# Hybrid decoder trunk: all input sums of the FFN's seven-product scheme emitted behind tile 1, and two more tiles per layer in that scheme

## Chip, core and metric

One core of a Trainium2 chip runs the whole program. The metric is device time in microseconds (us) for one launch, smaller is better.

## What is computed

Two layers, each a token mixer and a gated MLP, over 528 tokens of width 1024 (16 learned tokens are put in front of 512), in float32. The change touches the MLP:

```
h = h + ffn(rmsnorm(h));   out = rmsnorm(h) without the first 16 tokens
ffn(x): u = causal_dwconv3(x @ w_up) + b        # 1024 -> 2 x 2816
        gate, val = split(u)
        (silu(gate) * val) @ w_down             # 2816 -> 1024
```

## The kernel before

Data lie with features on partitions: a tile is 128 features by 528 tokens, worked on in two halves of 264 (in layer 1 two of 258, because the first tokens are dropped). Each float32 operand of a matrix product is split in two float32r parts, a high one (a ScalarE copy) and a low one (the rest), and each product is three matmuls: high by high, high by low, low by high. `split` (L420 to L427) makes the low part on VectorE by one subtraction, or, with `by_dma`, as a negated copy on ScalarE followed by a DMA from GpSimd's queue (POOL) that adds the source onto it.

The MLP of a layer has 22 FFN tiles. Tile j needs gate column block j and value column block 22 + j of `w_up`. In the plain scheme (`up_pair`, L1026) that is two units of 8 x 3 matmuls for each half, 96 in all. Tiles in `FAST` use `up_fast` (L1070) with `pair_products` (L377): a Winograd form of a 2 x 2 block product, in which seven products of 4 x 3 matmuls (84) take the place of eight. It needs four sums of the inputs, T1 to T4, which depend on the layer only, and sums of the four weight blocks, which each tile makes anew: the items `a` (blocks as they are), `b` and `c` (each 1024 columns, two additions of 512 columns apiece on VectorE, L292 to L296) and `d` (512 columns). The order of the seven products is B11, B21, T1, T2, B22, T3, T4.

The input sums are made by `sum_pair` (L1044), one call for each of four pairs of feature tiles. A call adds high and low parts back together for two feature tiles (L1049), makes T1 and T2 (L1055, L1056) and T3 and T4 (L1059, L1060), and splits each two of them with `by_dma` into `th` and `tl`. All four pairs are needed in the middle of product T1. Before, pair 0 is emitted behind tile 1, pairs 1 and 2 behind tile 2, pair 3 behind tile 3; the first fast tile is tile 4.

Tiles 0 and 1 run as one block of four units: first half of all four, then second half of all four. Emptying a tile means: copy out of PSUM and first tap (ScalarE), two more taps (VectorE, L1000), SiLU, a multiplication (L1022) and a split into `ah` and `al`. The tiles fall in five groups (`GROUPS`). The down projection of a group (8 row tiles, each two halves of 4 x 3 matmuls) runs inside the next group's fast tiles, as many rows in each as `DOWNS` says; the last group's down projection stands at the end of the layer, and of its first four units the products with the last activation tile are put last.

Working buffers `t` of the MLP are seven (`TM`, by `big`): a tile being emptied takes four, a `sum_pair` call four, of which the two that are split by DMA are free when that DMA has landed. `ah` and `al` have eight buffers (L1023). Weight tiles come through three `raw` buffers, are cut (`prep`, L265) three items ahead of the one taken, into four pairs `wh`, `wl`.

TensorE and SyncE run in the order of the program. On the other engines a planner in the framework puts ready instructions in order, by their place in the program, on its own costs; each queue then runs strictly in that order.

Of the kernel before, what the change touches and what calls it, by code (L numbers as in the profile page):

```python
# [19 lines left out]
KD = D // P  # L20
# [10 lines left out]
NFF = 22  # L31

GROUPS = ((0, 4), (4, 8), (8, 12), (12, 16), (16, 22))
FAST = range(4, 21)
DOWNS = ((), (2, 2, 2, 2), (2, 2, 2, 2), (2, 2, 2, 2), (2, 2, 2, 1, 1, 0))
TM = 7
Q0 = 12
MAXH = 2
# [55 lines left out]
def hybrid_trunk_kernel(ctx, tc, x, w_in, w_out, w_up, w_down, par, pre_in, lru_w, kon, msk, rope, out):  # L94
# [105 lines left out]
    raw_src, items = [], []  # L200
# [4 lines left out]
        group[f"x{j}"], group[f"y{j}"], group[f"s{j}"] = [M_LX + j], [M_LY + j], [M_RG + j]  # L205
    orders = [[m for k in o.split() for m in group[k]] for o in (ORDER, ORDER1)]

    def plain(src, kn, ring="raw"):
        raw_src.append((src, kn, ring))
        items.append(("p" if ring == "raw" else "q", len(raw_src) - 1, kn))  # L210

    for l in range(DEPTH):
        for m in orders[l]:
            plain(w_in[l, m], KD)
        for m in range(KD):
            plain(w_out[l, m], KD)

        for g, (k0, k1) in enumerate(GROUPS):
            rows = iter(range(KD))
            for i, j in enumerate(range(k0, k1)):  # L220
                down = [next(rows) for _ in range(DOWNS[g][i] if g else 0)]
                if j in FAST:
                    raw_src.extend((w_up[l, r], KD, "raw") for r in (j, NFF + j))
                    ri = len(raw_src) - 2
                    items.extend((k, ri, KD) for k in "ab")
                    for q, m in enumerate(down):
                        plain(w_down[l, m, :, slice(*GROUPS[g - 1]), :], 4, "rd")
                        if q == 0:
                            items.append(("c", ri, KD))
                    if not down:  # L230
                        items.append(("c", ri, KD))
                    items.append(("d", ri, KD))
                else:
                    plain(w_up[l, j], KD)
                    plain(w_up[l, NFF + j], KD)
        for m in range(KD):
            plain(w_down[l, m, :, k0:k1, :], k1 - k0)
    raws, ready, sums = {}, {}, {}
# [256 lines left out]
    def whole(hi, lo):  # L495
        return lambda t0, n: (hi[:, t0:t0 + n], lo[:, t0:t0 + n])
# [406 lines left out]
    def layer(l):  # L903
# [122 lines left out]
        def up_pair(j):  # L1026
            us = {}

            def ev(key, m):

                def f(i, t0, n, ps):
                    if key not in us:
                        us[key] = new_u()
                    u, c = us[key]
                    S.copy(u[:, 2 + t0:2 + t0 + n], ps[:, 0:n])
                    o = max(t0, c0)
                    tap(u, c, m, o, t0 + n, ps[:, o - t0:n])
                return f
            return [(None, ev("g", j), lambda: gate(j, us)), (None, ev("v", NFF + j), lambda: value(j, us))]
# [4 lines left out]
        def sum_pair(a):  # L1044

            y = []
            for k in (2 * a, 2 * a + 1):
                y.append(big())
                V.tensor_tensor(y[-1][:, 0:2 * hn], xh[:, k, h0:T].bitcast(F32), xl[:, k, h0:T].bitcast(F32), op=ALU.add)  # L1049
            (b11, b12), (b21, b22) = ((t[:, 0:hn], t[:, hn:2 * hn]) for t in y)  # L1050
            for i in (0, 2):
                t = big()
                p0, p1 = t[:, 0:hn], t[:, hn:2 * hn]
                if i == 0:
                    V.tensor_tensor(p0, b11, b12, op=ALU.subtract)  # L1055
                    V.scalar_tensor_tensor(p1, p0, -1.0, b22, op0=ALU.mult, op1=ALU.subtract)  # L1056
                    t2 = p1
                else:
                    V.tensor_tensor(p0, b22, b12, op=ALU.subtract)  # L1059
                    V.scalar_tensor_tensor(p1, t2, -1.0, b21, op0=ALU.mult, op1=ALU.subtract)  # L1060
                split(t[:, 0:2 * hn].rearrange("p (h t) -> p h t", t=hn), *(x[:, a, i:i + 2, 0:hn] for x in tsum),
                      by_dma=True)
# [7 lines left out]
        def up_fast(j, halves):  # L1070
            us = {k: new_u() for k in "gv"}
            ug, uv = (us[k][0][:, 2 + h0:2 + T] for k in "gv")

            def evac(what, ps):
                p = ps[:, 0:hn]
                if what == "c11":
                    S.copy(ug[:, 0:hn], p)
                elif what == "u":
                    S.copy(ug[:, hn:2 * hn], p)
                elif what == "q5":  # L1080
                    S.activation(uv[:, hn:2 * hn], p, AF.Copy, scale=-1.0)
                elif what == "c11b":
                    V.tensor_tensor(ug[:, 0:hn], ug[:, 0:hn], p, op=ALU.add)
                elif what == "c12":
                    V.tensor_tensor(ug[:, hn:2 * hn], ug[:, hn:2 * hn], p, op=ALU.add)  # L1085
                    u, c = us["g"]
                    tap(u, c, j, c0, T, u[:, 2 + c0:2 + T])
                    gate(j, us)
                elif what == "v":
                    V.tensor_tensor(uv[:, hn:2 * hn], uv[:, hn:2 * hn], p, op=ALU.subtract)  # L1090
                else:
                    S.activation(uv[:, 0:hn], p, AF.Copy, scale=-1.0)
                    u, c = us["v"]
                    tap(u, c, NFF + j, c0, T, u[:, 2 + c0:2 + T])
                    value(j, us)
            cut_at = (len(halves) + 1) // 2

            def between(i):
                for f in (halves[:cut_at], halves[cut_at:])[i]:
                    f()  # L1100
            pair_products(xs_fast, KD // 2, hn, evac, between)

        def down_halves(m, xs):

            w = []

            def f(t0, n):
                if not w:
                    w.append(take())
                ps = ps_mm.tile([P, 512], F32, tag="mm", name=nm("mm"))  # L1110
                product(w[0], xs, t0, n, range(len(xs)), ps, True, True)
                resid(m)(0, t0, n, ps)
            return [lambda t0=t0, n=n: f(t0, n) for t0, n in hd]

        for g, (k0, k1) in enumerate(GROUPS):
            rows = iter(range(KD))
            prev = [whole(*act[k]) for k in range(*GROUPS[g - 1])] if g else []
            for i, j in enumerate(range(k0, k1)):
                halves = [f for _ in range(DOWNS[g][i] if g else 0) for f in down_halves(next(rows), prev)]
                if j in FAST:  # L1120
                    up_fast(j, halves)
                else:
                    if j == 0:
                        run_units([u for i_ in range(2) for u in up_pair(i_)], xs_norm, hv, first=4)
                    elif j > 1:
                        run_units(up_pair(j), xs_norm, hv)
                    if j in (1, 2, 3):
                        for a in {1: (0,), 2: (1, 2), 3: (3,)}[j]:
                            sum_pair(a)

        def final(t0, n):
# [27 lines left out]
    with tc.manual_schedule(engines={mybir.EngineType.PE, mybir.EngineType.SP}):  # L1159
# [132 lines left out]
        for l in range(DEPTH):  # L1292
            layer(l)
# [106 lines left out]
```

## Time and profile before

| | us |
|---|---|
| median of 3 runs (lowest, highest) | 1287.32 (1286.71, 1287.97) |
| the profiled execution, its span | 1288.41, 1286.5 |
| TensorE busy | 1258.5 (98%) |
| VectorE busy | 988.6 (77%) |
| ScalarE busy | 752.0 (58%) |
| GpSimd busy | 79.5 (6%) |
| mean granted TensorE clock | 0.987 |

Engines are named PE (TensorE matmul), DVE (VectorE), ACT (ScalarE), POOL (GpSimd), SP (SyncE). Times within the run are from the start of the span. In a row, `out<-in` are the tiles' names, L is the line, and what stands in brackets or behind a second bar is idle time ahead of it with what ended it. Listed durations on DVE and ACT overlap a little: the next one starts 0.06 to 0.1 us before the end of the one ahead.

### The profile page before, as it was taken

Reading aid. Unit: us, or ns where it says so; the run is one execution under the profiler, and the core shown is the slowest. Engines: PE = TensorE matmul, PEld = TensorE weight load, DVE = VectorE, ACT = ScalarE, POOL = GpSimd, SP = SyncE. Lnnn points to the kernel's source line nnn. Section 1 sums busy time; section 2 is a strip of 40 time slices with the busy share of each in tenths; the row PEclk is TensorE's granted clock in tenths of the full one; section 3 lists DMA queues with packets and bytes.
Section 4 is the critical chain, followed back from the end, with each engine's and each line's share of the span. In section 5 each row is a group of like instructions: output and inputs, shape, how many; then the busy total and the mean of one; then the engine's idle time right before and its main releaser. Section 6 shows DMA issues by size and latency. Waiting matters only on the chain.

```text
span 1286.5 us, 25758 instructions
## 1 busy us (share of the span) xinstructions
PE 1258.5 (98%) x10244; PEld 1245.9 (97%) x10244; DVE 988.6 (77%) x1946; ACT 752.0 (58%) x1442; POOL 79.5 (6%) x179
## 2 busy tenths in 40 slices
PE   9999999999899999999999999999999999999997
PEld 8999999999899999999999999999989999999996
DVE  7987676468788888887588767764896888888865
ACT  6665555347666666666456645553684666666652
POOL 0000000001211111100000000000021111111000
PEclk8999999999899999999999999999998999999998
DMA  5322312324555445544232223122265555555422
GB/s 197 98 78 67 100 50 66 99 67 122 126 132 132 131 128 136 132 124 115 75 99 67 66 66 100 50 83 66 87 136 139 132 132 131 132 137 135 111 88 74
DMA packets 53240, 135.32 MB, mean 105 GB/s; under 512 B 5632, under 2 KB 12288, under 8 KB 53120
## 3 DMA queue, kind: packets, MB, share of 16 engines
q1 hardware_dynamic: 39424, 110.46, 27.5%
q0 software_dynamic: 12544, 21.06, 9.7%
q10 hardware_dynamic: 1152, 2.16, 0.5%
q8 instruction: 80, 1.31, 0.4%
q14 instruction: 40, 0.33, 0.1%
HBM read 110.51 MB, written 2.10 MB: 88 GB/s over the span
## 4 chain that ended last, share of the span: by engine, by line
PE 86%; DVE 6%; ACT 3%; DMA 3%; issue 1%; SPq 0%; POOL 0%; DVEq 0%; ACTq 0%; POOLq 0%
PE mm L130 63%; PE mx L130 23%; DMA tl<-t 2%; DVE t L1000 1%; PE mx L137 1%; DVE wl L427 1%; DVE t L567 1%; DVE t L1138 0%; DMA raw<-in_w_in_dram 0%; DVE sc L591 0%; ACT wh L421 0%; ACT th L421 0%; DMA mk<-in_msk_dram 0%; DVE t L870 0%; ACT sc L674 0%
## 5 line engine op out<-in xcount | busy, mean ns | idle before, releaser
L130 PE MATMUL mm<-xh,wh 128*128 128x264 f32 (+1 forms) x1424 | 417.9, 293 | 0.8 <-ACT xh L421 0.8
L130 PE MATMUL mm<-xl,wh 128*128 128x264 f32 (+1 forms) x1424 | 404.3, 284 | 0.7 <-DVE xl L427 0.3
L130 PE MATMUL mm<-xh,wl 128*128 128x264 f32 (+1 forms) x1424 | 403.4, 283 | 0.0
L130 PE MATMUL mm<-ah,wh 128*128 128x264 f32 (+2 forms) x960 | 273.2, 285 | 0.0
L130 PEld LDWEIGHTS mm<-xl,wh 128*128 128x128 f32 x1424 | 268.8, 189 | 3.7 <-issue 1.9
L130 PE MATMUL mm<-al,wh 128*128 128x264 f32 (+2 forms) x960 | 272.4, 284 | 0.0
L130 PE MATMUL mm<-ah,wl 128*128 128x264 f32 (+2 forms) x960 | 272.1, 283 | 0.0
L130 PEld LDWEIGHTS mm<-xh,wh 128*128 128x128 f32 x1424 | 268.5, 189 | 3.6 <-issue 2.0
L130 PEld LDWEIGHTS mm<-xh,wl 128*128 128x128 f32 x1424 | 268.6, 189 | 0.2 <-DVE wl L1195 0.2
L427 DVE TENSOR_TENSOR wl<-raw,wh 128x1024 fp32r<-128x1024 f32 (+2 forms) x168 | 182.5, 1088 | 82.2 <-ACT wh L421 81.7
L421 ACT CAST wh<-raw 128x1024 fp32r<-128x1024 f32 (+2 forms) x168 | 158.3, 942 | 149.2 <-PE mm L130 143.6
L130 PEld LDWEIGHTS mm<-ah,wh 128*128 128x128 f32 x960 | 182.0, 190 | 0.1
L130 PEld LDWEIGHTS mm<-al,wh 128*128 128x128 f32 x960 | 181.9, 189 | 0.1
L130 PEld LDWEIGHTS mm<-ah,wl 128*128 128x128 f32 x960 | 181.9, 189 | 0.0
L1000 DVE SCALAR_TENSOR_TENSOR t<-t,pr,t 128x528 f32<-128x528 f32 (+1 forms) x176 | 132.7, 757 | 11.1 <-ACT t L1005 5.1
L130 PE MATMUL mx<-th,wh 128*128 128x264 f32 (+1 forms) x408 | 117.2, 287 | 0.0
L130 PE MATMUL mx<-th,wl 128*128 128x264 f32 (+1 forms) x408 | 116.6, 286 | 0.0
L130 PE MATMUL mx<-tl,wh 128*128 128x264 f32 (+1 forms) x408 | 116.3, 285 | 0.0
L1005 ACT ACTIVATE t<-t,pr 128x528 f32<-128x528 f32 (+1 forms) x68 | 56.0, 823 | 58.5 <-DVE t L1085 56.5
L427 DVE TENSOR_TENSOR wl<-ss,wh 128x1024 fp32r<-128x1024 f32 x68 | 83.0, 1221 | 4.6 <-ACT wh L421 1.8
L425 POOL DMA_DIRECT2D wl<-rd x64 | 56.6, 884 | 448.6 <-ACT wl L424 384.4
L130 PEld LDWEIGHTS mx<-tl,wh 128*128 128x128 f32 x408 | 78.3, 192 | 0.0
(231 smaller groups left out, 2170.9 us busy)
## 6 DMA issues: line engine op xcount, KB each, us to landing
raw<-in_w_up_dram SPq DMA_DIRECT2D x88, 512.0 KB, 3.6
raw<-in_w_in_dram SPq DMA_DIRECT2D x52, 512.0 KB, 3.6
rd<-in_w_down_dram SPq DMA_DIRECT2D x64, 256.0 KB, 2.7
wl<-rd POOLq DMA_DIRECT2D x64, 256.0 KB, 3.6
raw<-in_w_out_dram SPq DMA_DIRECT2D x16, 512.0 KB, 3.5
raw<-in_w_down_dram SPq DMA_DIRECT2D x16, 384.0 KB, 3.1
hT<-in_x_dram SPq DMA_DIRECT2D x4, 528.0 KB, 5.4
t<-in_rope_dram ACTq DMA_DIRECT2D x8, 264.0 KB, 3.3
```

What stands on the lines that cost most here:

```text
L130: PE.matmul(o, a, b, start=start, stop=stop, **kw)
L137: PE.transpose(o, a, ident[0:n, 0:n])
L421: S.copy(hi, src)
L425: G.dma_start(lo, src, accum_op=ALU.add)
L427: V.tensor_tensor(lo, src, hi.bitcast(F32), op=ALU.subtract)
L567: V.tensor_tensor(o, a, b, op=ALU.mult)
L1000: V.scalar_tensor_tensor(c[:, 0:cn], u[:, i + c0:i + c0 + cn], pr[l][:, w + i:w + i + 1], c[:, 0:cn], op0=ALU.mult, op1=ALU.add)
L1005: S.activation(c[:, a - c0:b - c0], src, AF.Identity, bias=pr[l][:, C_FB + m:C_FB + m + 1], scale=pr[l][:, C_FW + 3 * m + 2:C_FW + 3 * m + 3])
```

## The change

Fast tiles become 3 to 21 (from 4 to 20). All four `sum_pair` calls are emitted behind tile 1. The weights of the plain tiles 1 and 2 are split with `by_dma`. The last group's rows of the fourth group's down projection go 2, 1, 1, 2, 1, 1 over tiles 16 to 21 instead of 2, 2, 2, 1, 1, 0.

```diff
-FAST = range(4, 21)
-DOWNS = ((), (2, 2, 2, 2), (2, 2, 2, 2), (2, 2, 2, 2), (2, 2, 2, 1, 1, 0))
+FAST = range(3, 22)
+DOWNS = ((), (2, 2, 2, 2), (2, 2, 2, 2), (2, 2, 2, 2), (2, 1, 1, 2, 1, 1))
+SENT = (1, 2)
...
-    def plain(src, kn, ring="raw"):
+    def plain(src, kn, ring="raw", by_dma=False):
         raw_src.append((src, kn, ring))
-        items.append(("p" if ring == "raw" else "q", len(raw_src) - 1, kn))
+        items.append(("q" if by_dma else "p", len(raw_src) - 1, kn))
...
-                        plain(w_down[l, m, :, slice(*GROUPS[g - 1]), :], 4, "rd")
+                        plain(w_down[l, m, :, slice(*GROUPS[g - 1]), :], 4, "rd", True)
...
-                    plain(w_up[l, j], KD)
-                    plain(w_up[l, NFF + j], KD)
+                    plain(w_up[l, j], KD, by_dma=j in SENT)
+                    plain(w_up[l, NFF + j], KD, by_dma=j in SENT)
...
-                    if j in (1, 2, 3):
-                        for a in {1: (0,), 2: (1, 2), 3: (3,)}[j]:
+                    if j == 1:
+                        for a in {1: (0, 1, 2, 3)}[j]:
                             sum_pair(a)
```

## Rows read from the trace of the kernel before

**Rows 1.** The page: busy time by engine, and the chain that ended last, by engine
```profile
PE 1258.5 (98%) x10244; PEld 1245.9 (97%) x10244; DVE 988.6 (77%) x1946; ACT 752.0 (58%) x1442; POOL 79.5 (6%) x179
...
PE 86%; DVE 6%; ACT 3%; DMA 3%; issue 1%; SPq 0%; POOL 0%; DVEq 0%; ACTq 0%; POOLq 0%
```
**Rows 2.** PE's waits, whole run: in total, times, longest
```profile
PE mm L130 <- DMA tl<-t: 9.0, 2, 4.8
PE mm L130 <- ACT th L421: 2.5, 2, 1.5
```
**Rows 3.** Timeline of PE, layer 0, tile 4: start, duration, [idle before]
```profile
324.19 0.28 PE L130 MATMUL mx<-xh,wh 128*128 128x264 f32 x1
...
329.41 0.39 PE L130 MATMUL mm<-th,wh 128*128 128x264 f32 x1 [1.04 <-ACT th L421]
334.03 0.59 PE L130 MATMUL mm<-tl,wh 128*128 128x264 f32 x1 [4.23 <-DMA tl<-t]
```
**Rows 4.** Timeline of PE, layer 1, tile 4
```profile
957.23 0.28 PE L130 MATMUL mx<-xh,wh 128*128 128x258 f32 x1
...
967.98 0.58 PE L130 MATMUL mm<-tl,wh 128*128 128x258 f32 x1 [4.78 <-DMA tl<-t]
```
**Rows 5.** The chain in order of time: start, duration, what
```profile
309.81 5.58 DMA tl<-t
330.23 3.75 DMA tl<-t
...
599.54 38.01 PE mm L130 x312
...
1228.60 37.09 PE mm L130 x312
```
**Rows 6.** Busy time by stretch: length, then engines, granted clock, DMA share, GB/s
```profile
293.30:333.30 40.00, 35.46 (x291) 35.04 (x289) 39.52 (x64) 32.42 (x61) 8.62 (x16) 0.99 0.59 140
...
334.03:339.24 5.21, 5.21 (x23) 5.21 (x24) 0.69 (x1) 1.29 (x3) 0.02 (x1) 0.50 0.61 103
360.20:376.20 16.00, 16.00 (x134) 16.00 (x134) 13.63 (x21) 9.99 (x17) 1.86 (x4) 1.00 0.51 133
568.80:582.00 13.20, 13.20 (x111) 13.20 (x110) 12.60 (x19) 8.58 (x14) 1.00 (x3) 1.00 0.43 117
599.40:611.00 11.60, 11.60 (x98) 11.60 (x97) 7.62 (x11) 7.05 (x13) 0.00 (x0) 1.00 0.45 137
967.98:974.12 6.14, 6.14 (x28) 6.14 (x29) 0.86 (x2) 1.28 (x3) 0.00 (x0) 0.50 0.71 134
```
**Rows 7.** Timeline of DVE, layer 0, tiles 0 to 4
```profile
294.47 1.56 DVE L1000 SCALAR_TENSOR_TENSOR t<-t,pr,t 128x528 f32<-128x528 f32 x2
...
299.18 0.71 DVE L1049 TENSOR_TENSOR t<-xh,xl 128x528 f32<-128x528 f32 x1
299.81 0.70 DVE L1022 TENSOR_TENSOR t<-t,t 128x528 f32<-128x528 f32 x1
...
306.61 0.42 DVE L1056 SCALAR_TENSOR_TENSOR t<-t,t 128x264 f32<-128x264 f32 x1
...
308.26 1.21 DVE L427 TENSOR_TENSOR wl<-raw,wh 128x1024 fp32r<-128x1024 f32 x1
309.39 0.68 DVE L292 TENSOR_TENSOR ss<-raw 128x512 f32<-128x512 f32 x1
...
328.14 0.43 DVE L1056 SCALAR_TENSOR_TENSOR t<-t,t 128x264 f32<-128x264 f32 x1
```
**Rows 8.** Timeline of ACT, layer 0, second half of tiles 0 and 1
```profile
292.25 1.05 ACT L421 CAST wh<-raw 128x1024 fp32r<-128x1024 f32 x1 [1.79 <-PE mm L130]
...
296.15 0.57 ACT L1005 ACTIVATE t<-mm,pr 128x264 f32<-128x264 f32 x1
```
**Rows 9.** The page's DMA issues: number, size of each, median us to landing
```profile
wl<-rd POOLq DMA_DIRECT2D x64, 256.0 KB, 3.6
```
**Rows 10.** Timeline of DVE, layer 0: the last low part of tile 21
```profile
615.88 0.71 DVE L427 TENSOR_TENSOR al<-t,ah 128x528 fp32r<-128x528 f32 x1 [0.75 <-ACT ah L421]
```

## Prediction

> **What bounds the kernel now.** I read the page's busy times and chain first. PE is busy 98% and is 86% of the chain [rows 1], so the end moves by matmuls left out and by PE's waits. PE's waits over the whole run come next. Nearly all of them are one event, twice: the wait for the DMA that finishes `tl`, 9.0 us, and just ahead of it the wait for `th`, 2.5 us [rows 2]. PE's timeline puts both in the first fast tile of each layer. Tile 4 starts at 324.19, reaches the last quarter of product T1, and goes on with `tl` of pair 3 at 334.03 [rows 3]; in layer 1 at 967.98, for a tile that started at 957.23 [rows 4]. Behind that wait, in which PE did nearly nothing, the table of stretches shows the granted clock at 0.50, the lower of the two levels (1.2 GHz), for 5.21 us in layer 0 and 6.14 us in layer 1 [rows 6]. What makes the sums late is in the first row of the same table: from 293.3 to 333.3 DVE is busy 39.52 us of 40, while ACT has 32.42 [rows 6]. So this stage is bound by DVE, then by the chain behind the last sum. From the end of pair 3's T2 (328.14 + 0.43 = 328.57) to the matmul at 334.03 it takes 5.46 us: ACT's two copies, the issue on POOL, and a transfer of 3.75 us [rows 3, 5, 7].
>
> **The change part by part.** I count against the profiled execution, 1288.41 us (span 1286.5); the median of the runs is 1.09 us less.
>
> *Tile 21.* It loses 12 of 96 matmuls. A run of 312 takes 38.01 us, so 0.1218 us each in layer 0, and 37.09 us, 0.1189 each, in layer 1 [rows 5]: 1.46 + 1.43 = 2.89 us off PE. The cover is DVE. A fast tile with two down rows (16.0 us of PE) costs DVE 13.63 us; one with one row (13.2 us) shows 12.60 [rows 6]. Tile 21 left DVE idle for four of its 11.60 us; now it has the load of its neighbours, and 0.5 us of slack. The last activation was there at 615.88 + 0.71 = 616.6 [rows 10]; tile 21 ended near 611.2 (96 matmuls behind 599.54, where the run starts [rows 5]), and the 60 matmuls put ahead of it last 7.3 us, to 618.5. A first tap over 528 columns instead of 264 takes some 0.3 of the 1.9 us left.
>
> The new order of down rows adds a wait. The last row now runs in tile 21, and until it is through, the four old activation tiles hold half of the eight `ah`/`al` buffers, so tile 20's activation has none until 12 matmuls (1.46 us) before tile 21 ends. Then a cast and a subtraction of 0.71 [rows 10] follow, at most 1.05 + 0.71 = 1.8 us [rows 8, 10], and it is needed 12 matmuls into the down projection. That is 2.9 us from release to need, less what is queued behind the waiting cast on ACT (tile 21's own copies). Bounds 0 and 1.46 us; I take 0.3 a layer, near the free end. Tails: 2.89 - 0.6 = 2.3 us gained.
>
> *Tile 3 and the sums together.* Tile 3 has no down rows, so a whole fast tile, 84 matmuls, lies between its use of pair 3 and tile 4's: 84 x 0.1218 = 10.23 us, and 9.99 in layer 1. The changed kernel breaks even if pair 3 lands at 334.03 - 10.23 = 323.8, in layer 1 at 957.99. PE itself would be there sooner: tile 3 starts 96 matmuls before 324.19, at 312.5, and needs pair 3 34 matmuls later, at 316.6.
>
> When does it land? DVE's list, by the pitch of starts, 0.08 under the listed durations [rows 7]: emptying tiles 0 and 1, eight taps of 0.74 and four operations of 0.63, 8.4; three pairs of 2 x 0.63 + 4 x 0.34, 7.9; pair 3 to its T2, 1.9; item `a` of tile 3, 1.1; item `b`, 2.3. That is 21.6 us from the first tap at 294.47, so 316.1, and with the 5.46 us behind it 321.6. Without item `b` in between it is 319.3; with tile 2's emptying ahead of the last sums (4.2 us more) it is 325.8. The buffers say the same by another way: a tap of tile 1 started at 296.15 only when the taps begun at 294.47 had freed a `t` [rows 7, 8], so seven are too few already. With four calls in a row, pair 3's last `t` has to wait for pair 0's landing, 309.81 + 5.58 = 315.39 [rows 5]; two operations and the 5.46 us make 321.6 too. I take 322.0, since ACT also gets 2 x 0.95 us of negated copies for tile 2's weights in this stretch. Gain against break-even: 1.8 us, in layer 1 (the same chain 633.95 us later) 2.0. PE's wait stays as long as it was, some 5.4 us, and I leave the slow stretch as it is.
>
> What is late next is DVE's backlog. Tile 3's DVE work grows from about 6.5 (two cuts and an emptying) to 13.63 less four additions of 0.4 for the down rows, 12.0; tile 2's two cuts, 2.3, go to the DMA. So DVE has 3.2 us more to do in the stretch that it fills, and only 2.4 us per tile to win back after it. I charge 1.0 a layer (0 to 3.2). Starts: 0.8 + 1.0 = 1.8 us gained.
>
> *Weights of tiles 1 and 2 by DMA.* Tile 2's gate weights are cast from 292.25 [rows 8]; the negated copy ends near 294.3, the issue is some 0.9, and a transfer of twice 256 KB takes between 3.6 (the row for one) and 7.2 [rows 9]: 297.9 to 302.4, against a need at 300.8 + 0.24. I cost it at nothing; uncovered it is up to 1.4 us a unit; tile 1's likewise. They also hold their `raw` buffer until the landing, so tile 3's second load starts up to 5 us later; its sums are not due before 315.
>
> A rule that speaks against this: the Trainium skill (SBUF — State Buffer, section "SBUF: two separate sides") says that a DMA from GpSimd's queue can't write its descriptors while VectorE holds the shared port in a 2-port mode. The trace has such DMAs inside the stretch where DVE is full, and they landed in 3.75 and 5.58 us [rows 5, 6], the second with weight loads beside it. By the rule each could be late by one DVE operation, 1.2 us, which would make the sum 2.4 us longer; by the rows nothing is added.
>
> **Sum.** 2.3 + 1.8 = 4.1 us: 1288.41 - 4.1 = 1284.3 profiled, 1283.2 as a median.
>
> **The rivals.**
>
> *The buffers give a second wait (slower).* The sums' first operations are ready early and come first in the program, so they take the seven `t`. Tile 2 can't be emptied until they let go, and tile 3 needs four more: its T2 goes into the bank whose first content has to be copied to a `t`. Once pair 3 has landed, DVE still owes tile 2's emptying, 4.2 us, and PE waits for it and a copy (0.4), 4.6 us a layer. For it: the tap at 296.15 [rows 8]. Against it: that DVE runs other work while buffers are short, 39.52 of 40 [rows 6]. It decides from about 2 us a layer, the gain of both parts. Time: starts 2 x 3.8 lost, tails 2.3 gained: 1292.6.
>
> *The sums come in time (faster).* Pair 3 at 319.3, 4.5 us better a layer; the wait shrinks to 2.7 us and the clock stays at 2.4 GHz. The slow stretches cost 5.21 - 24 x 0.1218 = 2.3 and 6.14 - 28 x 0.1189 = 2.8 us [rows 6], so 2 x 4.5 + 5.1 + 2.9 = 17 us: 1270.3. Against it: DVE and ACT would have to follow the ideal order.
>
> *POOL's queue comes late.* It now carries eight sums and four weight tiles in the same 30 us; tile 1's and 2's weights make PE wait 1.5 us a layer: 1286.2.
>
> *The tail gives nothing.* Tile 20's and 21's activations come late by what the matmuls save: 1286.
>
> *The sums don't move.* The planner may still run tile 2's emptying first; that is the end 325.8 of the forecast.
>
> **How the numbers follow.** Forecast 0.38 (its own range 1276 to 1291, landing from 319.3 to 325.8, the backlog 0 to 3.2, the tail 0 to 1.46); second wait 0.20; sums in time 0.13; POOL late 0.17; no gain at the tail 0.12. A difference of 0.2%, 2.6 us, is what a measurement of this kernel can tell: faster is below 1284.7, slower above 1289.9. Faster: 0.27 of the forecast, 0.13, 0.06 and 0.04, 0.50. Slower: 0.17 of the second wait, 0.03 of POOL, 0.03 of the others, 0.23. Same: 0.27. The range 1272 to 1292 leaves out about half of the two outer rivals.
>
> **What would show it.** Right: PE has 48 matmuls less; its longest wait is still one for `tl`, now in tile 3, ended near 322 and 956; tile 4 starts near 329 to 331; the down projection at the layer's end follows tile 21 without a gap over 0.5 us. Wrong: a PE wait that ACT's copies out of PSUM end (second wait); pair 3 before 320 with the clock at full behind it; waits in tile 1 or 2 for `wl`; a wait for `ah` or `al` of tile 20 or 21. If both waits are gone and the time still is no better, the reading of the tails fails.

## The result, and the profile after

The changed kernel takes 1298.43 us in the median of three runs (1296.53 to 1299.26); the kernel before takes 1287.32. The ratio is 1.0083, with a 95% interval of 1.0061 to 1.0106. The change makes the kernel slower by some 11 us. The forecast was 1283.2, in a range from 1272 to 1292, so it failed in sign and in range. The profiled execution is the shortest of the three, 1296.53 us with a span of 1294.7; it is 8.1 us above that of the kernel before, while the medians are 11.1 apart.

Busy times and chain of the changed kernel, to be read beside [rows 1]:
```profile
PE 1258.4 (97%) x10196; PEld 1243.8 (96%) x10196; DVE 998.7 (77%) x1974; ACT 763.2 (59%) x1450; POOL 86.2 (7%) x187
...
PE 86%; DVE 6%; DMA 3%; ACT 3%; issue 2%; POOL 0%; SPq 0%; DVEq 0%; ACTq 0%; POOLq 0%
```
The 48 matmuls are gone, but PE is busy as long as before: fewer instructions, more of them at a lower clock. The 6.8 us more at half the clock (end of this section) make up at most 3.4 us of the 5.8 that 48 matmuls take; what makes up the rest stays open. PE's waits over the whole run say where (in total, times, longest), against [rows 2]:
```profile
PE mm L131 <- ACT t L1006: 8.5, 4, 3.1
PE mm L131 <- DMA wl<-raw: 5.5, 4, 1.8
PE mm L131 <- DMA tl<-t: 4.1, 2, 2.9
```
Two waits, for `tl` and `th`, were 11.5 us; now three are 18.1. The first is for a PSUM bank: PE can't write until ACT has copied the bank's content to a `t` buffer. The second is for the weights that the DMA now finishes. The third is the old wait for pair 3. PE's timeline puts them in order, in layer 0 and, in the last three rows, in layer 1:
```profile
310.10 0.39 PE L131 MATMUL mm<-xh,wl 128*128 128x264 f32 x1 [0.98 <-DMA wl<-raw]
...
320.57 0.59 PE L131 MATMUL mm<-xh,wh 128*128 128x264 f32 x1 [3.14 <-ACT t L1006]
...
324.39 0.39 PE L131 MATMUL mm<-th,wh 128*128 128x264 f32 x1 [0.81 <-ACT t L1006]
...
327.34 0.59 PE L131 MATMUL mm<-tl,wh 128*128 128x264 f32 x1 [1.20 <-DMA tl<-t]
...
957.91 0.39 PE L131 MATMUL mm<-xh,wh 128*128 128x258 f32 x1 [3.08 <-ACT t L1006]
...
961.68 0.58 PE L131 MATMUL mm<-th,wh 128*128 128x258 f32 x1 [1.46 <-ACT t L1006]
...
967.22 0.58 PE L131 MATMUL mm<-tl,wh 128*128 128x258 f32 x1 [2.93 <-DMA tl<-t]
```
Pair 3 is there at 327.3 and 967.2, where the forecast had 322 and 956. The table of stretches, for the first and the last row of [rows 6]:
```profile
293.30:333.30 40.00, 33.87 (x247) 32.72 (x246) 31.98 (x54) 29.44 (x52) 8.97 (x14) 0.91 0.67 147
...
958.70:972.40 13.70, 9.31 (x42) 8.69 (x41) 9.62 (x14) 8.85 (x18) 2.44 (x2) 0.50 0.79 177
```
DVE, busy for 39.52 of the 40 us before, is busy for 31.98. It is no longer what bounds the stage, and the stage still got longer. And TensorE has the lower of its two levels (1.2 GHz) for 13.7 us in one piece in layer 1, from 0.8 us behind the first bank wait to 5 us behind the wait for pair 3. Outside the start and the end of the run, the clock record holds 17.1 us at that level before and 23.9 us after.

### The profile page after: what moved, and what is told of

Its sections match the earlier page's. It is cut to its first block, busy times and chain, and to the rows that moved or that the text cites. A ratio compares the mean times of both kernels' runs of the same rounds, so it can differ in the third digit from the quotient of the medians.

```text
span 1294.7 us, 25732 instructions
## 1 busy us (share of the span) xinstructions
PE 1258.4 (97%) x10196; PEld 1243.8 (96%) x10196; DVE 998.7 (77%) x1974; ACT 763.2 (59%) x1450; POOL 86.2 (7%) x187
## 3 DMA queue, kind: packets, MB, share of 16 engines
q0 software_dynamic: 13696, 25.25, 11.3%
## 4 chain that ended last, share of the span: by engine, by line
PE 86%; DVE 6%; DMA 3%; ACT 3%; issue 2%; POOL 0%; SPq 0%; DVEq 0%; ACTq 0%; POOLq 0%
PE mm L131 60%; PE mx L131 24%; DMA tl<-t 2%; DMA wl<-raw 1%; PE mx L138 1%; DVE wl L428 1%; DVE t L568 1%; DVE t L1001 1%; DMA raw<-in_w_in_dram 0%; DVE t L1139 0%; DVE t L1050 0%; DVE sc L592 0%; ACT wh L422 0%; DVE t L871 0%; ACT sc L675 0%
## 5 line engine op out<-in xcount | busy, mean ns | idle before, releaser
L131 PE MATMUL mm<-xh,wh 128*128 128x264 f32 (+1 forms) x1328 | 393.6, 296 | 7.0 <-ACT t L1006 6.2
L131 PE MATMUL mm<-xh,wl 128*128 128x264 f32 (+1 forms) x1328 | 379.1, 285 | 5.5 <-DMA wl<-raw 5.5
L131 PE MATMUL mm<-xl,wh 128*128 128x264 f32 (+1 forms) x1328 | 379.4, 286 | 0.4 <-DVE xl L428 0.3
L131 PEld LDWEIGHTS mm<-xh,wh 128*128 128x128 f32 x1328 | 253.0, 190 | 10.3 <-ACT t L1006 6.6
L131 PEld LDWEIGHTS mm<-xh,wl 128*128 128x128 f32 x1328 | 252.9, 190 | 6.5 <-DMA wl<-raw 6.3
L131 PEld LDWEIGHTS mm<-xl,wh 128*128 128x128 f32 x1328 | 253.1, 191 | 3.4 <-issue 1.9
L131 PE MATMUL mx<-th,wh 128*128 128x264 f32 (+1 forms) x456 | 131.2, 288 | 1.2 <-DVE t L1091 1.2
L131 PE MATMUL mx<-th,wl 128*128 128x264 f32 (+1 forms) x456 | 130.4, 286 | 0.0
L131 PE MATMUL mx<-tl,wh 128*128 128x264 f32 (+1 forms) x456 | 130.0, 285 | 0.0
L131 PEld LDWEIGHTS mx<-th,wh 128*128 128x128 f32 x456 | 87.3, 191 | 1.8 <-DVE t L1091 1.8
```

The source lines that it names most:

```text
L131: PE.matmul(o, a, b, start=start, stop=stop, **kw)
```

## The experiments

Times are medians; the ratio is to the kernel before on the same chip, with its 95% interval. The waits are PE's, in us over the run: for weights (`wl`, by the DMA's or DVE's finish), for a bank (ACT's copy to `t`), and for sums (`th`, `tl`). early_own2_tail also waits 2.7 us for ACT's copies of another bank (L1077), the others at most 1.0; the kernels in which tile 3 takes seven products wait 1.0 to 1.2 us for DVE at a third (L1091). The last column is the time at the lower clock level between start and end.

| kernel | us | ratio | weights | bank | sums | low clock |
|---|---|---|---|---|---|---|
| before | 1287.3 | 1 | 0 | 0 | 11.5 | 17.1 |
| changed | 1298.4 | 1.0083 [1.0061, 1.0106] | 5.5 | 8.5 | 4.1 | 23.9 |
| tail_only | 1285.2 | 0.9977 [0.9967, 0.9986] | 0 | 0 | 11.9 | 13.7 |
| start_only | 1297.9 | 1.0083 [1.0069, 1.0096] | 5.5 | 9.6 | 3.2 | 27.3 |
| sent_only | 1309.4 | 1.0157 [1.0134, 1.0179] | 13.4 | 0 | 11.2 | 37.5 |
| sent1_only | 1294.1 | 1.0049 [1.0033, 1.0064] | 3.3 | 0 | 11.7 | 23.9 |
| no_sent | 1295.7 | 1.0061 [1.0047, 1.0074] | 0 | 10.7 | 7.8 | 23.9 |
| no_tile3 | 1299.4 | 1.0084 [1.0070, 1.0098] | 13.3 | 6.7 | 0 | 27.3 |
| neither | 1283.9 | 0.9964 [0.9950, 0.9977] | 0 | 11.2 | 0 | 13.7 |
| sums_only | 1287.1 | 0.9995 [0.9986, 1.0005] | 0 | 11.3 | 0 | 17.1 |
| sums_own2 | 1276.7 | 0.9913 [0.9899, 0.9928] | 1.8 | 0 | 0 | 0 |
| no_sent_own2 | 1289.0 | 1.0010 [1.0000, 1.0019] | 8.1 | 0 | 7.0 | 20.5 |
| own_gate_tail | 1279.5 | 0.9929 [0.9915, 0.9942] | 0 | 6.3 | 0 | 13.7 |
| tail_pair3early | 1279.5 | 0.9935 [0.9920, 0.9950] | 0 | 2.3 | 2.3 | 6.8 |
| tail_0112 | 1283.0 | 0.9959 [0.9945, 0.9973] | 0.6 | 2.7 | 3.1 | 13.7 |
| early_own2_tail | 1281.4 | 0.9951 [0.9939, 0.9964] | 0.6 | 2.2 | 0 | 10.2 |
| sums_own2_tail | 1274.1 | 0.9897 [0.9883, 0.9911] | 1.9 | 0 | 0 | 3.4 |

### Is the tail's part right?

tail_only is the kernel before with tile 21 and its down rows alone; start_only is the changed kernel without them.
```diff
-FAST = range(4, 21)          # tail_only, against before
+FAST = range(4, 22)
-DOWNS = (..., (2, 2, 2, 1, 1, 0))
+DOWNS = (..., (2, 1, 1, 2, 1, 1))
-FAST = range(3, 22)          # start_only, against the change; DOWNS as before
+FAST = range(3, 21)
```


> The kernel before with only the tail of the change: fast tiles 4 to 21, down rows 2, 1, 1, 2, 1, 1; input sums and weights as before. Theory T (the tails gain what the forecast counted, 24 matmuls less a small charge): 2.3 to 2.9 us under the kernel before, 1284.5 to 1285.0. Rival (tile 20's and 21's activations come late by what is saved): within 1 us of the kernel before. If T holds, all of the loss, and 2 to 3 us more, belongs to the starts of the MLPs.

> The change without tile 21: tile 3 by seven products, all sums behind tile 1, both tiles' weights sent. Theory (the tail's 2.6 us are separate from the start's loss): the changed kernel's ratio 1.0083 and 2.6 us more, 1300 to 1303 us on a kernel before of 1288, with the same waits in tiles 2 to 4 as the changed kernel. Rival (tile 21 lost its gain inside the change, since its sums or copies come at a layer's end that is late): 1297 to 1299.5.

Alone it gives 2.6 us, as the theory had it. Inside the change the medians don't show it: start_only's 1297.9 is the rival's figure. But the intervals (1.7 and 2.9 us each way) don't exclude it, and the trace of the changed kernel shows it against the one before. In layer 0 all work is 3.7 us late at tile 6 (it starts at 368.06, before at 364.38) and 2.4 us late behind tile 21, where layer 1's FFN starts. In layer 1 it is 9.6 us late at tile 6 (1007.85, before 998.20) and 8.2 at the end. That is 1.2 and 1.4 us gained. start_only, which has neither gain, also has 3.4 us more at the lower clock than the changed kernel, so the two don't differ by the tail alone. So the loss lies in the start of each layer, and it is some 13.5 us there by the medians (10.9 in the profiled execution).

### The sent weights, alone and in the change

```diff
+SENT = (1, 2)                # sent_only, against before; sent1_only: SENT = (1,)
...
-                    plain(w_up[l, j], KD)
+                    plain(w_up[l, j], KD, by_dma=j in SENT)
...
-SENT = (1, 2)                # no_sent, against the change
+SENT = ()
```


> The changed kernel with the weights of tiles 1 and 2 split on VectorE again. Theory B (seven t buffers: the sums hold them, tile 2 is emptied late, PE waits for PSUM banks, then for pair 3): the waits for wl go (5.5 us in the trace, and the slow stretch of 3.4 us behind the one in layer 1), the waits ended by ACT's copies stay or grow by the two cuts that DVE gets back: 1290 to 1294, still slower than before. Rival W (the late weights push everything behind them, and the rest follows from that): back to 1284 to 1287, waits for banks under 3 us in all.

> The kernel before with only the weights of tiles 1 and 2 split by DMA. Theory W: PE waits for wl as in the changed kernel, some 2.7 us a layer, and nothing gives it back: 1291 to 1294. Theory B: the same waits, but tile 2's two cuts (2.3 us) leave the full DVE stretch, so pair 3 lands up to 2.3 us earlier and the wait for tl shrinks by part of it: 1286 to 1290.

> The kernel before with only tile 1's weights finished by the accumulating transfer; tile 2's stay with the vector engine. With both tiles' weights sent, the time rose by 21.6 us. Theory (tile 2's are the dear ones: its raw buffers are held by tile 1's transfers, its copies start late and its matmul waits 5 us a layer, with the low clock behind it): 1288 to 1293 us, waits for wl of at most 2 us a layer. Rival (the transfers themselves are dear, each unit the same): half of it, 1297 to 1301 us.

Taken out of the change they give 2.7 us, which the intervals don't tell from nothing; 1295.7 is above what either side had expected. Put into the kernel before, they cost 20 us, more than either theory had; tile 1's alone cost 6.5 (1294.1, 1 us above its theory's range). PE's waits in sent_only:
```profile
PE mm L131 <- DMA wl<-raw: 13.4, 4, 5.3
PE mm L131 <- DMA tl<-t: 8.0, 2, 4.3
```
The relief of DVE bought next to nothing: PE's wait for `tl` was 9.0 and is 8.0, and in sent1_only it is 9.1. The same part costs 20 us in one place and 3 in the other, so the parts aren't additive.

### Both taken back

no_tile3 and neither undo tile 3's seven products in the change, the second one the sent weights as well.
```diff
-FAST = range(3, 22)          # no_tile3 and neither
+FAST = range(4, 22)
-SENT = (1, 2)                # neither only
+SENT = ()
```


> The changed kernel with tile 3 back in eight products; sums, sent weights and tile 21 as in the changed kernel. Theory (tile 3 is the dear part also beside ring buffers and sent weights): 2.9 us of matmuls more, but the kernel with the sums alone was at 1287, tile 21 gives 2.6 back and the sent weights cost 2.7 when the sums are early, so 1285 to 1290 us against 1298. Rival (the sent weights are as dear as they were alone, 21.6 us, whenever tile 3 does not hide their lateness behind its own wait): 1296 to 1306.

> The changed kernel with both taken back, tile 3 by seven products and the sent weights; sums behind tile 1 and tile 21 by seven products stay. Taking back one of them alone gave at most 2.7 us. Theory (the two delays lie beside each other: either alone holds the sums' stage up by about as much as both): both taken back give 12 to 15 us, 1283 to 1287 us, with only the wait for t L1006 of the kernel that moves the sums alone. Rival (they add up as measured one by one, 2.7 and nothing): 1294 to 1298.

Tile 3 taken back alone gives nothing (no_tile3's theory failed, its rival's range held), the sent weights alone 2.7 us, both together 15 us (1.0083 to 0.9964). So each of the two is enough to make the start late by about as much as both. With neither, tile 3 costs 12.5 us (no_sent against neither); with tile 3 in eight products, the sent weights cost 15 (no_tile3 against neither). A single-part undo, read by itself, would have acquitted both. no_tile3 shows why the weights are so dear. Its chain in order of time, ahead of the wait in tile 2 (start, duration, what):
```profile
299.07 4.61 DMA wl<-raw
...
303.73 3.52 DMA raw<-in_w_up_dram
...
308.87 0.96 ACT wl L425
...
310.11 0.15 POOL wl L426
```
ACT's timeline at the same place:
```profile
307.27 1.06 ACT L422 CAST wh<-raw 128x1024 fp32r<-128x1024 f32 x1 [1.14 <-DMA raw<-in_w_up_dram]
308.23 0.64 ACT L1018 ACTIVATE t<-t 128x528 f32<-128x528 f32 x1
308.77 1.05 ACT L425 ACTIVATE wl<-raw 128x1024 fp32r<-128x1024 f32 x1
```
And PE's timeline, at the matmul that needs the transfer:
```profile
315.72 0.59 PE L131 MATMUL mm<-xh,wl 128*128 128x264 f32 x1 [4.79 <-DMA wl<-raw]
```
There are three `raw` buffers. A sent tile keeps its own until the accumulating transfer has landed (299.07 + 4.61 = 303.68), so the next weight load starts at 303.73; in the kernel before, the load in that place started at 294.58:
```profile
294.58 0.33 SPq L249 DMA_DIRECT2D raw<-in_w_up_dram  x1
```
The cast that needs this load waits on ACT, and in the order that the planner wrote for ACT the negated copy of tile 2's second weight tile stands behind that cast. So the transfer that PE waits for is issued at 310.11. In the changed kernel, whose load in that place starts at 301.85, ACT's order in this stretch has one whole-tile cast less, the negated copy starts at 304.19, and PE waits 0.98 us instead of 4.79.

### The sums and the buffers

sums_only moves the four sums of the kernel before behind tile 1, and nothing else. sums_own2 empties tile 2 into the buffers `rd` (made wide enough for it) and `ss`, which are idle then, instead of the ring of seven `t`.
```diff
-                    if j in (1, 2, 3):
-                        for a in {1: (0,), 2: (1, 2), 3: (3,)}[j]:
+                    if j == 1:                                # both
+                        for a in (0, 1, 2, 3):
...
-            u, c = big(), big()
+            u, c = (own(tag, 2, ...) if tag else big() for _ in range(2))   # sums_own2
...
-                        us[key] = new_u()
+                        us[key] = new_u({"g": "rd", "v": "ss"}[key] if j == 2 else None)
```


> The kernel before with only the four input sums emitted behind tile 1; the first fast tile is still tile 4, so pair 3 is needed 11.7 us later than in the changed kernel. Theory B: pair 3 lands near 322 to 327, so the wait for tl (4.2 and 4.8 us) goes, but tile 2 is emptied as late as in the changed kernel and tile 3's units wait for banks, 3 to 7 us a layer: 1283 to 1292, with waits ended by ACT's copies of PSUM in tile 3. Rival (the early sums are free when nobody needs them early): both waits and the slow stretches behind them go, 1270 to 1276.

> The kernel with the four sums behind tile 1 and the first fast tile 4, with one edit: tile 2 is emptied into buffers of its own (the two rd and the two ss, which nothing else uses yet), not into the seven t. Theory B (tile 2's buffers come behind the sums' in the ring of t, so its PSUM banks stay full): the waits of 5.5 and 6.3 us at tile 3's start go, pair 3 is in time anyway, the clock stays at full: 11 us of waits and some 5 us of slow clock less, 1269 to 1273. Rival Q (not the buffers: DVE and ACT are full, and the copies out of PSUM stand behind the sums' work in any case): waits of 3 us or more a layer stay, 1281 to 1287.

The sums alone change nothing: the wait for `tl` is gone and one for a bank, as long, has come. PE's longest wait in sums_only, and the copy on ACT that ends it:
```profile
PE mm L130 <- ACT t L1005: 11.3, 2, 6.0
```
```profile
317.44 0.57 ACT L1005 ACTIVATE t<-mm,pr 128x264 f32<-128x264 f32 x1 [0.66 <-DMA tl<-t]
```
The copy out of PSUM has no `t` until a transfer of the sums lands and lets one go. The row shows 0.66 us of that; the rest lies in the order of ACT's queue, which has tile 2's copies behind the sums. Its first copy, in sums_only and, with buffers of its own, in sums_own2:
```profile
316.40 0.38 ACT L1035 COPY t<-mm 128x264 f32<-128x264 f32 x1 [0.17 <-issue]
```
```profile
304.02 0.38 ACT L1035 COPY rd<-mm 128x264 f32<-128x264 f32 x1 [0.70 <-PE mm L130]
```
PE's longest wait in this stage of sums_own2 is then
```profile
PE mm L130 <- DVE wl L427: 1.5, 2, 0.8
```
and the time falls by 10.3 us, with the clock at its upper level from the start of the run to its end part. The theory's 1269 to 1273 was too good by 4 us; no single wait that is left in this stage is over 0.8 us, and they are mostly for casts on DVE and ACT.

### Tile 3 by itself

no_sent_own2 is no_sent with the gate half of tile 2 in `rd` (`ss` is used by a fast tile 3). own_gate_tail is the same with tile 3 in eight products.
```diff
-                        us[key] = new_u()
+                        us[key] = new_u("rd" if j == 2 and key == "g" else None)   # both
-FAST = range(3, 22)
+FAST = range(4, 22)                                                            # own_gate_tail
```


> The changed kernel without the DMA-split weights (tile 3 fast, all sums behind tile 1), with tile 2's gate half emptied into the two rd buffers. Theory B: the waits of 5.2 and 6.1 us for a bank in tile 3 shrink to under 2 us; pair 3 is needed near 316 and lands by DVE's list at 319 to 323, so a wait for tl of 3 to 6 us stays, with its slow stretch: 1285 to 1291. Rival Q: no change, 1294 to 1297.

> The kernel of 1289.0 us (no sent weights, all sums behind tile 1, tile 2's gate half emptied into buffers of its own, tile 21 by seven products) with one thing changed: tile 3 goes back to eight products. Theory (tile 3 asks for its casts and for the sums some 10 us before the vector engine has them, 8.1 us of waits for wl and 7.0 for tl and the low clock behind them): without it 1274 to 1279 us, though 24 x 0.12 = 2.9 us of matmuls are added. Rival (the value half, still emptied into the ring, is what costs): 1283 to 1289, with a wait for t L1005 that the kernel with both halves in buffers of their own does not have.

The buffers give 6.7 us against no_sent, and tile 3 in eight products gives 10 more (1.0010 to 0.9929; the 1279.5 is at the upper end of what the theory had), though 24 matmuls (2.9 us) come back with it. PE's waits in no_sent_own2, and the cut of tile 3's weights that the first of them is for:
```profile
PE mm L131 <- DVE wl L428: 8.1, 2, 4.3
PE mm L131 <- DMA tl<-t: 7.0, 3, 3.5
```
```profile
318.50 1.22 DVE L428 TENSOR_TENSOR wl<-ss,wh 128x1024 fp32r<-128x1024 f32 x1
```
Neither wait is in own_gate_tail, whose one wait left, 6.3 us, is for a bank of the value half, still in the ring. So tile 3 by seven products has two needs, its own weight sums and pair 3, both at a time at which DVE and the transfers haven't got that far.

### The order of the sums, and the best kernel

```diff
-                        for a in {1: (0,), 2: (1, 2), 3: (3,)}[j]:   # with tile 21, tile 3 in eight:
+                        for a in {1: (0,), 2: (1, 2, 3), 3: ()}[j]:  # tail_pair3early, early_own2_tail
+                        for a in {1: (0, 1), 2: (2, 3)}[j]:          # tail_0112
+                        for a in {1: (0, 1, 2, 3)}[j]:               # sums_own2_tail
```
The two kernels with own2 in their name empty tile 2 as sums_own2 does.

> The kernel before with the tail of the change (fast tiles 4 to 21, new down rows) and one more edit: pair 3's sum is emitted behind tile 2 with pairs 1 and 2, not behind tile 3. What made pair 3 late before is then its place behind tile 3's emptying on DVE. Theory B: pair 3 lands 4 to 7 us earlier, near its need at 328; tile 3's emptying comes 2 to 3 us later and its banks are needed only in tile 4's product B21: 1270 to 1277. Rival (DVE's total work sets the end of the stretch, whatever its order): another wait of 4 us or more takes its place, 1283 to 1286.

> As the run with pair 3 behind tile 2, but two pairs behind tile 1 and two behind tile 2. Theory B: eight t buffers' worth of sums stand ahead of tile 2's emptying, half as many as with four pairs, so the wait for a bank at tile 3's start is under 2 us, and pair 3 is in time: 1269 to 1275. Rival: the wait for a bank is as long as with four pairs (5 to 6 us a layer), 1283 to 1286.

> As the run beside it, but with only pair 0 summed behind tile 1 and pairs 1 to 3 behind tile 2. Theory (buffers of tile 2 and the order of the sums are two separate causes; with the own buffers the early sums of all four are what counts): the wait for tl of 1.4 us a layer that the same order left with ring buffers comes back, 1276 to 1279 us. Rival (the order behind tile 2 is as good once tile 2's results do not use the ring, because its units then come before the sums on the vector engine and the small waits of 0.8 us for tile 3's casts go): 1272 to 1274.5.

> The kernel before with all four sums behind tile 1, tile 2's results emptied into buffers of their own, and tile 21 by seven products; tile 3 stays in eight and no weights are sent. Theory (the parts add up: the buffers' run gained 11.1 us, tile 21 alone 2.6): 1288.0 - 11.1 - 2.6 = 1274 us, 1272 to 1276, with no wait for tl and no wait for t L1005 above 1 us. Rival (the end of the layer becomes bound by what the earlier start brings forward, so tile 21 gives nothing): 1276 to 1278. Against the run without sent weights and with tile 3 by seven products (1289.0) it says what tile 3 costs.

With the buffers as they are, moving only pair 3 forward, behind tile 2, gives 5.4 us beyond the tail (0.9977 to 0.9935). With pair 1 moved forward too it is 2.3 us, and with all four behind tile 1 (neither) 1.7. So with seven `t`, a second pair behind tile 1 costs 3.1 us; the step from two to four, 0.6 us, is within the intervals. That the second pair costs by taking buffers from tile 2 is not shown: its waits for banks and sums are only 1.2 us longer, and 6.8 us more at the lower clock come with them. With all four the wait for a bank is the long one, 11.2 us. Both kernels came out slower than their theory had them. tail_0112 came out at its rival's figure, but without its rival's wait: 2.7 us for a bank, not 5 to 6 a layer. With buffers of its own for tile 2 the ranking turns round: the order behind tile 2 gains nothing by them (1281.4 beside 1279.5, outside both ranges; no run shows why), and all four sums behind tile 1 are 7 us better than it (0.9951 to 0.9897). That kernel, sums_own2_tail, is the fastest: 1274.1 us, 1.0% below the kernel before and 1.8% below the change. The two gains add up to the 1274 that was expected.

## Why the prediction was wrong

**The tails: right.** 2.3 us were forecast, 2.6 measured alone, with no wait at the down projection; in the change the traces have 1.2 and 1.4.

**The steps that failed: when pair 3 lands, and when PE comes to it.** The break-even rule was right. Layer 0's wait ended at 327.34 against 323.8, 3.5 us late, and tile 5 started 3.7 us later than before. In layer 1 all work was 2.4 us late already (its FFN starts at 912.42, before at 909.98), so break-even is 960.4; the wait ended at 967.22, 6.8 late, and tile 5 lost 7.2. These two losses, less the tails, are the difference of the profiled executions.

The prediction had PE ready for pair 3 at 316.6, so that only the landing counted. PE came to it at 327.34 - 1.20 = 326.14, in layer 1 at 967.22 - 2.93 = 964.29. That alone is 2.3 and 3.9 us behind break-even: by this sum the starts lose 6.2 us even with the forecast's landings, and the wait for pair 3 adds the last 1.2 and 2.9 us. The waits for `wl` had tile 3 start at 315.82 instead of 312.5; then came the two waits for a bank, 3.14 and 0.81 us, with 3.4 us at the lower clock between them. The prediction counted none of these in its sum.

The landing was wrong as well, 322.0 and 955.95. The changed kernel's chain has the forecast's own steps (start, duration, what; the last two rows are layer 1's):
```profile
311.49 5.56 DMA tl<-t
...
317.14 0.71 DVE t L1050
...
321.88 5.41 DMA tl<-t
...
948.79 5.52 DMA tl<-t
...
959.81 7.36 DMA tl<-t
```
and DVE's row of T2 of pair 3, with the row in which DVE waits for a buffer:
```profile
315.81 0.43 DVE L1056 TENSOR_TENSOR t<-t 128x264 f32<-128x264 f32 x1 [1.66 <-DMA tl<-t]
...
319.42 0.43 DVE L1057 SCALAR_TENSOR_TENSOR t<-t,t 128x264 f32<-128x264 f32 x1
```
That pair 3's last buffer waits for a landed transfer was foreseen, as a second way to 321.6: 315.39, two operations, then 5.46 us. Each term was too small. The transfer that frees the buffer landed at 317.05, 1.66 us later. From there to the end of T2 it was 2.80 us (319.85) instead of 0.75, since DVE's list holds five operations ahead of T2. ACT and POOL took 2.03 instead of 1.71, with two copies of tile 2 in between. The transfer took 5.41 us, where the row of before had 3.75 [rows 5]. Together that is 5.7 us, from 321.6 to 327.3. In layer 1 the last transfer, from its issue to its landing, took 7.36.

**DVE as the bound.** The stage was read as bound by DVE, from 39.52 of 40 us [rows 6]. That is a reading of the kernel before alone. The change made DVE idle by 8 us in the same stretch and the stage longer: buffers and transfers took over. So the argument against the first rival, that DVE ran other work while buffers were short, didn't carry over to a program that asks for four sums at once.

**The rivals.** What happened is nearest to the first, the buffers' second wait, which had 0.20 and 1292.6 us. Its bank wait is there, and sums_only and sums_own2 show that it is the ring of `t`: it costs 10 us in that pair, 6.7 in the change without sent weights, against the rival's 9.2. It expected the bank wait behind pair 3, but it came ahead of it and pair 3 was late as well. The waits for `wl` in tiles 1 and 2, the sign of the third rival, came with it, but not by its cause. POOL's queue wasn't full; in the changed kernel POOL stood idle before the transfer that PE waits for at 310.10, until ACT had made the negated copy:
```profile
305.55 0.86 POOL L426 DMA_DIRECT2D wl<-raw  x1 [7.45 <-ACT wl L425]
```
The forecast took the rivals as alternatives, and they came together.

**The weights by DMA, at nothing.** The bound of 1.4 us a unit was too low: the waits of the change go up to 1.8, those of no_tile3 to 5.0. (The lower end of that sum, 297.9, leaves out the 0.9 us of the issue; with it, it is 298.8. The bound doesn't hang on it.) The hold on `raw` was put at up to 5 us and measures 7.3 in the change (301.85 against 294.58). It was named and dismissed since tile 3's sums come later; what it reached, in no_tile3, was another instruction, the negated copy that stands in ACT's queue behind the cast of the late load. And the relief by tile 1's weights came where DVE had time: in the 10 us from 283 to 293 it is busy for 6.56 in the kernel before and 4.79 in sent1_only, while from 297 to 338, where the sums are made, sent1_only still has it busy for 39.72 us of 41.

**The clock.** The slow stretches were left as they were. They grew from 17.1 to 23.9 us. In the kernel before they are 6.8 us (332.4 to 339.2) and 10.2 us (963.9 to 974.1); the prediction's 5.21 and 6.14 are the parts behind the waits.

**The rule on GpSimd's DMAs.** The transfers did get longer, so the rule weighed in the prediction (the Trainium skill, SBUF — State Buffer, section "SBUF: two separate sides") had to be looked at again. It is about VectorE's operations in a 2-port mode. The 1.2 us that the prediction took for it is a TENSOR_TENSOR (L427 [rows 7]), and no run here shows that this one, or which other, runs in such a mode, so the 2.4 us had no support. If VectorE's work did hold the descriptors up, landings should be latest where it is busiest. The medians from issue to landing, of before, changed and sums_own2_tail for the stretch 300 to 335, go another way:
```profile
tl<-t POOLq DMA_DIRECT2D x8, 264.0 KB, 3.4
```
```profile
tl<-t POOLq DMA_DIRECT2D x8, 264.0 KB, 5.0
```
```profile
tl<-t POOLq DMA_DIRECT2D x8, 264.0 KB, 4.4
```
DVE's busy time from 293 to 333 is 39.2, 31.7 and 38.0 us in these three. The longest landing goes with the least busy DVE of the three, so nothing here speaks for the rule as the cause. It goes with sent weights on the same queue (no_sent, without them, has 4.0) and with sums issued close together (3.4 before, 4.0 in sums_only). These two aren't all: sums_own2_tail has 4.4 without sent weights. How busy the DMA engines are (0.59 of the time before, 0.67 in the change [rows 6 and the table of stretches above]) was not separated from them.

**What stays open.** How the 10 to 12.5 us that tile 3 costs without sent weights split between its weight sums and pair 3 was not measured, and why tile 3 costs nothing on top of the sent weights was read from the waits (no_tile3 has 20.0 us of them, the change 18.1, and 2.9 us of matmuls less), not tried by itself.

## What to carry to other kernels

Before moving work earlier, count the buffers that it will hold while it waits, and ask which later work empties its results into the same ring; giving that work other buffers was worth more here than every reordering. Price a transfer that takes over an engine's work by the buffers that it keeps until it lands, and follow the freed load through the queues to whatever stands behind its first user. And undo parts in pairs: two parts that each hold up the same stage look harmless one at a time.

## What the runs showed of the hardware

- The same 16 accumulating transfers from SBUF to SBUF, issued by POOL (`tl`, 264 KB each in layer 0, 258 KB in layer 1), took from 3.3 to 6.6 us from issue to landing in the kernel before (median 3.8) and from 3.4 to 8.1 us in the changed one (median 5.1). The 512 KB ones, in the changed kernel's page, take no longer than its 264 KB ones:
```profile
wl<-raw POOLq DMA_DIRECT2D x8, 512.0 KB, 5.0
```
- Much the same wait of PE went with and without a fall of the clock. In the changed kernel the wait for tile 1's weights leaves 1.87 us between two starts of matmuls in layer 0 (283.19 to 285.06), and the clock stays at 2.4 GHz; in layer 1 it leaves 2.04 us (919.23 to 921.27), and 3.4 us at 1.2 GHz follow.
- Four kernels (start_only, no_tile3, own_gate_tail, sums_own2_tail) have 3.4 us at 1.2 GHz between 645 and 662 us, behind the down projection of layer 0, where the kernel before and the changed one have none. PE's waits just ahead of it (0.5, 0.3 and 0.3 us) are the same in the kernel before, so they don't tell the two apart. The cause is open.
